# Value projection folded into the output projection's weights, with earlier loads, in a hybrid encoder layer

## The chip, the cores and the metric

The kernel runs on one core of a Trainium2 chip. The metric is the device time of one execution in microseconds. A core has a matrix engine (TensorE, PE in the profile; its weight loads are PEld), a vector engine (VectorE, DVE), a scalar engine (ScalarE, ACT), a general engine (GpSimd, POOL) and an engine that mostly starts transfers (SyncE, SP). Each works through its own list of instructions in order and waits for the others by semaphores. SBUF and PSUM are the memories on the core; PSUM takes the results of matmuls. Transfers (DMA) are issued by an engine, SP for the most part and ACT for some, and run beside the engines.

## The reference

One layer with two kinds of heads, for 2048 tokens of width 1024:

```python
h = rms_norm(x, g_mix_norm)
z = h @ w_in                       # mLSTM q, k, v, out-gate, gates | q-latent (256), kv-latent (128), rotary key (64)
y_a = mlstm_group(...)             # 4 heads, values of 128: convolution of q and k, chunked scans both ways
kv = (rms_norm(c_kv, g_ckv) @ w_ukv).reshape(B, S, 4, 128 + 128)
k_nope, v = kv[..., :128], kv[..., 128:]
s = q . k * scale                  # per head, over all 2048 keys; q and k normalised, 64 of 192 columns rotated
y_b = softmax(s) @ v               # 4 heads, values of 128
x = x + concat(y_a, y_b) @ w_out   # rows 512 to 1023 of w_out belong to y_b, 128 per head
h = rms_norm(x, g_ffn_norm)
x = x + relu(h @ w_ff1)**2 @ w_ff2
```

All is float32. A head's values are a linear map of the normalised latent, `v = cn @ Wv_h`, and the output multiplies a head's result by its 128 rows of `w_out`.

## The kernel before, in words

**Precision.** A float32 matrix product is made of three matmuls on a faster format: each operand is split into a high part (a cast on ACT, L53, or L56 with a gain) and a low part (source minus high, on DVE or POOL, L54, or L57 with a gain), and `mm3` (L68 to L71) adds high x high, high x low and low x high in PSUM. Lines L53 to L57 and L69 to L71 are thus the lines of helpers, and the tile names tell where in the program they are.

**The projection stage** (0 to about 458 us) takes the tokens in two halves of 8 tiles of 128. In each half come a block `rest` (gates and latents), then three blocks of 8 steps: the mLSTM values (`z_v`), its queries and keys with their convolution (`z_qk`: five steps on DVE into acc, a sigmoid sg on ACT, their product ot on DVE at L455, and for the keys transposes on PE, L464 and, for the last two columns, L476), and the out-gate (`z_o`: sigmoid vo on ACT, L495, a product on DVE, a store d_sg issued by ACT, L497). The weights of a block are 8 row blocks, each loaded into a raw tile by SP and split into wh and wl. Beside the blocks `tick` runs the latent attention's preparation for one token tile in four parts. mla_a1 normalises the latents (cn) and transposes them (cTh, cTl). mla_a2 multiplies them with the weights: the kv-latent with the 1024 columns of w_ukv (wukh, wukl), the q-latent with 768. mla_b1 copies the values out of PSUM (vn, L369), stores them in the DRAM tensor d_va (L371) and normalises queries and keys. mla_b2 transposes and stores queries and keys. Input tiles are loaded by SP (`load_x`, L147) into a pool of two buffers and transposed in `prep`. This stage's order on each engine is not written out: a scheduler lays the instructions down by a simulated timeline with priorities (`urgent`).

**The attention stage** (about 458 to 1120 us) is issued as written. It goes over 16 blocks, 4 heads x 4 groups of 512 queries, each of 16 scores (a score is 128 queries by 512 keys: five matmuls, L1090 to L1094, and a reduction on DVE, L1095). One loop of steps g (a score each, 16 per block) issues the scores, the softmax of four scores before (ACT), the transposes of the block before (PE, with casts on ACT and low parts on DVE), the products with the values (`pv`), and one piece of the mLSTM (`work`: a prelude for the gates, L628 to L718, then chunk by chunk). Loads and splits of keys, queries and values for what comes stand at fixed steps: `split_k` of the next head in its last group (two of the last three on POOL, one on DVE), `split_q` on POOL, and `load_v` and `split_v` once per head and quarter, 16 times in all, the low part on POOL. For head 0 the value splits are at steps 6, 8, 10 and 12.

**The output stage** (about 1120 to 2540 us) multiplies the joined results with w_out and then does the feed-forward part, with products of blocks that save multiplications. It reads rows 512 to 1023 of w_out twice, in `weights` and in `load_b2`.

## Time and profile before

| what | value |
|---|---|
| time, median of 3 runs | 2543.32 us (2542.84 to 2547.24) |
| the profiled execution's own time | 2542.08 us |
| its span | 2540.3 us |
| PE busy | 2523.7 us (99%), 12380 instructions |
| DVE, ACT, POOL busy | 1726.1 us (68%), 1293.7 us (51%), 380.7 us (15%) |
| DMA | 392.53 MB, mean 155 GB/s |

The span runs from the first to the last instruction of one profiled execution; the time of an execution is a little longer. A row of the timeline gives start, length, engine, line, operation, and output <- inputs, then partitions x elements and types; in brackets stands how long the engine was idle before and what ended that. A row of the groups ends with busy time, the mean length of one in ns, and the idle time ahead. A row of the waits gives the waiting instruction <- what it waited for: us in total, times, longest.

### The profile page before, as it was taken

The page shows a single profiled execution, that of the slowest core. Times are in us where ns is not written, and L with a number is a line of the kernel's source. Part 1 is how long each engine was busy: PE and PEld are TensorE (multiplying, and loading weights), DVE is VectorE, ACT ScalarE, POOL GpSimd, SP SyncE. Part 2 cuts the span into 40 slices and gives each one's busy share as a digit, 9 for nine tenths or more (in the row PEclk, how much of TensorE's full clock was granted, in tenths as well). Part 3 has the DMA queues.
Part 4 walks back from the last instruction along what each step waited for, and adds up shares of the span by engine and source line. Part 5 has one row for each costly group of instructions (what it writes and reads, how often), then busy time and mean ns, then how long its engine had stood idle before and what let it go on. Part 6 is the DMA issues. An engine that isn't in the chain of part 4 may idle for free. (4 is left out here: it accounts for less than half of the span.)

```text
span 2540.3 us, 35812 instructions
## 1 busy us (share of the span) xinstructions
PE 2523.7 (99%) x12380; PEld 2111.3 (83%) x12380; DVE 1726.1 (68%) x3286; ACT 1293.7 (51%) x2900; POOL 380.7 (15%) x428
## 2 busy tenths in 40 slices
PE   9999999999999999999999999999999999999999
PEld 7888888788888888888888888888888888888887
DVE  5585467766667667678788777977775577665433
ACT  6454444656767677674455555655554323332332
POOL 1211111223323332200000000000000232322000
PEclk9999999999999999999999999999999999999999
DMA  5434234355344343235786555654448544444552
GB/s 177 143 112 152 91 113 137 111 146 134 89 115 114 85 121 102 63 110 193 235 271 227 196 189 185 244 166 149 142 153 300 201 149 142 145 145 145 211 183 95
DMA packets 295931, 392.53 MB, mean 155 GB/s; under 512 B 32262, under 2 KB 176965, under 8 KB 295749
## 3 DMA queue, kind: packets, MB, share of 16 engines
q1 hardware_dynamic: 293284, 385.78, 48.0%
q10 hardware_dynamic: 2464, 4.46, 0.5%
q8 instruction: 97, 1.59, 0.3%
q14 instruction: 86, 0.70, 0.1%
HBM read 258.51 MB, written 131.64 MB: 154 GB/s over the span
## 5 line engine op out<-in xcount | busy, mean ns | idle before, releaser
L69 PE MATMUL pd<-w2h,uh 128*128 128x512 f32 x896 | 348.8, 389 | 0.1
L70 PE MATMUL pd<-w2l,uh 128*128 128x512 f32 x896 | 348.7, 389 | 0.0
L71 PE MATMUL pd<-w2h,ul 128*128 128x512 f32 x896 | 348.7, 389 | 0.0
L54 DVE TENSOR_TENSOR ul<-ur,uh 128x1024 fp32r<-128x1024 f32 x110 | 149.3, 1357 | 251.8 <-ACT uh L53 251.8
L53 ACT CAST uh<-ur 128x1024 fp32r<-128x1024 f32 x110 | 115.7, 1052 | 396.0 <-PE pd L70 382.4
L54 DVE TENSOR_TENSOR ptl<-ptp,pth 128x512 fp32r<-128x512 f32 x248 | 171.1, 691 | 190.0 <-ACT pth L53 188.9
L53 ACT CAST pth<-ptp 128x512 fp32r<-128x512 f32 x248 | 143.4, 578 | 157.7 <-PE ptp L1137 157.1
L2015 DVE TENSOR_TENSOR e<-pu,e 128x512 f32<-128x512 f32 x224 | 151.3, 689 | 88.7 <-PE pu L71 87.7
L69 PEld LDWEIGHTS pd<-w2h,uh 128*128 128x128 f32 x896 | 168.2, 188 | 35.4 <-DVE e L2015 0.5
L71 PEld LDWEIGHTS pd<-w2h,ul 128*128 128x128 f32 x896 | 168.2, 188 | 34.9
L70 PEld LDWEIGHTS pd<-w2l,uh 128*128 128x128 f32 x896 | 168.2, 188 | 34.8
L1106 ACT ACTIVATE p<-p,nm 128x512 f32<-128x512 f32 x256 | 185.8, 726 | 2.6 <-DVE nm L1099 2.6
L1095 DVE TENSOR_SCALAR_CACHE_REDUCE p<-ps 128x512 f32<-128x512 f32 x256 | 167.4, 682 | 15.2 <-PE ps L1094 15.1
L2179 POOL TENSOR_TENSOR r<-wr,r 128x512 f32<-128x512 f32 x48 | 81.5, 1697 | 621.1 <-DMA wr<-in_w 590.0
L69 PE MATMUL pz<-wh,hh 128*128 128x512 f32 (+1 forms) x384 | 149.5, 391 | 1.7 <-ACT vo L495 0.7
L71 PE MATMUL pz<-wh,hl 128*128 128x512 f32 (+1 forms) x384 | 150.0, 391 | 0.0
L70 PE MATMUL pz<-wl,hh 128*128 128x512 f32 (+1 forms) x384 | 149.2, 389 | 0.1
L2018 ACT ACTIVATE e<-e 128x512 f32<-128x512 f32 x128 | 80.9, 632 | 120.5 <-DVE e L2015 114.0
L1137 PE MATMUL ptp<-ident,p 128*128 128x128 f32 x992 | 130.6, 274 | 0.5 <-DVE ptl L54 0.3
L1137 PEld LDWEIGHTS ptp<-ident,p 128*128 128x128 f32 x992 | 113.6, 140 | 14.1 <-issue 1.4
L1090 PE MATMUL ps<-kh,qh 128*128 128x512 f32 x256 | 112.8, 441 | 2.4 <-DVE p L1095 2.4
L1883 ACT CAST r<-w1raw 128x512 fp32r<-128x512 f32 x104 | 64.6, 622 | 92.5 <-PE pu L71 92.5
(526 smaller groups left out, 6463.5 us busy)
## 6 DMA issues: line engine op xcount, KB each, us to landing
d_u<-e SPq DMA_DIRECT2D x224, 256.0 KB
ur<-d_u SPq DMA_DIRECT2D x110, 512.0 KB
wr<-in_w SPq DMA_DIRECT2D x96, 256.0 KB
w1raw<-in_w SPq DMA_DIRECT2D x42, 512.0 KB
raw<-in_w_in SPq DMA_DIRECT2D x48, 256.0 KB
r<-in_w SPq DMA_DIRECT2D x22, 512.0 KB
mb<-d_M SPq DMA_DIRECT2D x32, 256.0 KB
acc<-d_x SPq DMA_DIRECT2D x16, 512.0 KB
```

Source lines behind the costliest of these rows:

```text
L53: r = nc.scalar.copy(hi, src)
L54: (eng or nc.vector).tensor_tensor(lo, src, hi.bitcast(F32), op=ALU.subtract)
L69: nc.tensor.matmul(out, ah, bh, start=first, stop=False, skip_group_check=more)
L70: nc.tensor.matmul(out, ah, bl, start=False, stop=False, skip_group_check=more)
L71: nc.tensor.matmul(out, al, bh, start=False, stop=last, skip_group_check=more)
L1090: nc.tensor.matmul(o, qh[:, qs], kh, start=True, stop=False)
L1095: nc.vector.tensor_scalar(p, o, SCALE, None, op0=ALU.mult, op1=ALU.max, accum_out=maxes[b, a][:, j:j + 1])
L1106: nc.scalar.activation(p, p, AF.Exp, bias=maxes[b, a], accum_out=dens[b][:, a, j:j + 1])
L1137: nc.tensor.transpose(pt[:, k, :], p[:, k * P:(k + 1) * P], c.ident)
L2015: nc.vector.tensor_tensor(out, o, t, op=ALU.add)
L2018: nc.scalar.activation(t, t, AF.Relu)
L2179: nc.gpsimd.tensor_tensor(R, wr, R, op=ALU.subtract)
```

## The change

Since a head's result is softmax(s) times cn times Wv_h, and the output then multiplies by that head's rows of w_out, the kernel now attends with the normalised kv-latent itself (128 wide, the same for all four heads) and multiplies the head's result with `Wv_h @ w_out[head's rows]`, a 512 x 1024 matrix d_wv that it forms once.

- Values: d_va, its copies (vn) and its stores go. mla_a2 stores the latent cn (d_cn, 128 columns) from ACT's queue, and has one product of 512 columns for the keys instead of two for keys and values. Attention loads and splits the 4 quarters of d_cn once, at steps 2 to 8 and 16 to 22, and uses them for all heads.
- `value_rows()`, a generator called once a step in the second half from step n = 11 on, forms d_wv: it loads w_ukv again, scales its value columns with the gain (ACT), transposes them (four on PE), splits them into wvh and wvl, and then multiplies head by head with the pieces of w_out: 8 products of three matmuls, in psM tiles named pm. The pieces 0, 2, 4, 6 are split into a pair wh, wl of the weights' pool, the pieces 1, 3, 5, 7 into the pair acc, sg of the convolution's. The results are copied by ACT to ot or zc and stored from ACT's queue.
- The output stage reads d_wv where it read rows 512 to 1023 of w_out.
- Input tiles: three buffers instead of two. Tiles 8 to 10 are loaded at step i = 3 of the first half's last block, ahead of the weights that follow, and tiles 11 to 15 three tiles ahead.
- In the attention stage one split_k of a head change goes from POOL to DVE, and the mLSTM's chunk loads move: the first four into the prelude, the later ones a step ahead.

```diff
-    c.d_va = dr.tile([S, 512], F32, name="d_va")
+    c.d_cn = dr.tile([S, P], F32, name="d_cn")
+    c.d_wv = dr.tile([NH * P, D], F32, name="d_wv")
...
-        xp = pool("a_x", 2, "right")
+        xp = pool("a_x", 3, "right")
...
+        wvh = gp.tile([P, NH, P], F32R, name="wvh")
+        wvl = gp.tile([P, NH, P], F32R, name="wvl")
...
-                raw = rp.tile([P, 512], F32, name="raw")
-                cs = slice(j * 512, (j + 1) * 512)
-                nc.sync.dma_start(raw, c.w_ukv[:, cs])
-                split(nc, wukh[:, cs], wukl[:, cs], raw, gcq[:, 2:3])
+                raw = load_ukv(j)
+                cs = slice(j * 256, (j + 1) * 256)
+                split(nc, *[w[:, cs].rearrange("p (h d) -> p h d", h=2) for w in (wukh, wukl)],
+                      raw[:, :, 0, :], gcq[:, 2:3])
+
+        def load_ukv(j):
+            raw = rp.tile([P, 512], F32, name="raw")
+            nc.sync.dma_start(raw, c.w_ukv[:, j * 512:(j + 1) * 512])
+            return raw.rearrange("p (h t d) -> p h t d", h=2, t=2)
+
+        def value_rows():
+            raws = [load_ukv(j) for j in range(2)]
+            yield
+            for raw in raws:
+                nc.scalar.activation(raw[:, :, 1, :], raw[:, :, 1, :], AF.Copy, scale=gcq[:, 2:3])
+            pt = psT.tile([P, 4, P], F32, name="pt")
+            for h in range(NH):
+                nc.tensor.transpose(pt[:, h, :], raws[h // 2][:, h % 2, 1, :], c.ident)
+            split(nc, wvh, wvl, pt)
+            yield
+            for _ in range(3):
+                yield
+            pieces, parts = {}, {}
+            homes = [(wp.tile([P, 512], F32R, name="wh"), wp.tile([P, 512], F32R, name="wl")),
+                     [ep.tile([P, 520], F32R, name=name, bufs=1)[:, 0:512] for name in ("acc", "sg")]]
+
+            def load(n):
+                if n < 2 * NH:
+                    h, j = divmod(n, 2)
+                    pieces[n] = rp.tile([P, 512], F32, name="raw")
+                    nc.sync.dma_start(pieces[n], c.w_out[512 + h * P:512 + (h + 1) * P, j * 512:(j + 1) * 512])
+
+            def part(n):
+                if n < 2 * NH:
+                    parts[n] = homes[n % 2]
+                    split(nc, *parts[n], pieces.pop(n))
+                    load(n + 5)
+
+            for n in range(5):
+                load(n)
+            yield
+            part(0)
+            part(1)
+            yield
+            for grp in ((0,), (1,), (2, 3), (4, 5), (6, 7)):
+                for n in grp:
+                    h, j = divmod(n, 2)
+                    o = psM.tile([P, 512], F32, name="pm")
+                    mm3(nc, o, wvh[:, h, :], wvl[:, h, :], *parts.pop(n), True, True)
+                    w = ep.tile([P, 520], F32, name=("ot", "zc")[j])[:, 0:512]
+                    nc.scalar.copy(w, o)
+                    nc.scalar.dma_start(c.d_wv[h * P:(h + 1) * P, j * 512:(j + 1) * 512], w)
+                for n in grp:
+                    part(n + 2)
+                yield
...
-                pk.append(o)
+            zr, ms3, ch, cl, cn = mla_env[t]
+            nc.scalar.dma_start(c.d_cn[t * P:(t + 1) * P, :], cn[:, 256:384])
+            pq = []
+            pk = psM.tile([P, 512], F32, name="pm")
+            mm3(nc, pk, ch[:, 2, :], cl[:, 2, :], wukh[:, 0:512], wukl[:, 0:512], True, True)
...
-            vn = mp.tile([P, NH, DV], F32, name="vn")
-            for j in range(2):
-                nc.scalar.copy(vn[:, 2 * j:2 * j + 2, :],
-                               pk[j].rearrange("p (h d) -> p h d", h=2)[:, :, NOPE:])
-            nc.sync.dma_start(c.d_va[tok, :], vn.rearrange("p h d -> p (h d)"))
...
+            elif 8 <= t < 13:
+                xts[t + 3] = load_x(t + 3)
...
+            rows = value_rows()
...
+                    if half and n >= 11:
+                        next(rows, None)
+                    if half == 0 and blk == 2 and i == 3:
+                        for t in range(8, 11):
+                            xts[t] = load_x(t)
...
+        for ch in grp:
+            if ch > 4:
+                ld[ch - 4] = mlstm_v(c, ch - 4), mlstm_k(c, ch - 4)
         yield
         for k, ch in enumerate(grp):
             new = back[ch - 1] = advance(1, NT - 1 - ch, outs[k])
             if ch > 4:
                 nc.sync.dma_start(c.d_C[ch - 1], new)
-                ld[ch - 4] = mlstm_v(c, ch - 4), mlstm_k(c, ch - 4)
...
-        def load_v(h, j):
-            raw = vraw[h, j] = rp.tile([P, 512], F32, name="raw").rearrange("p (k d) -> p k d", k=4)
-            nc.sync.dma_start(raw, c.d_va[j * 512:(j + 1) * 512, h * DV:(h + 1) * DV].rearrange(
-                "(k p) d -> p k d", p=P))
-
-        def split_v(h, j):
-            raw = vraw.pop((h, j))
+        def load_v(j):
+            raw = vraw[j] = rp.tile([P, 512], F32, name="raw").rearrange("p (k d) -> p k d", k=4)
+            nc.sync.dma_start(raw, c.d_cn[j * 512:(j + 1) * 512, :].rearrange("(k p) d -> p k d", p=P))
+
+        def split_v(j):
+            raw = vraw.pop(j)
             vh = vp.tile([P, 4, DV], F32R, name="vh")
             vl = vp.tile([P, 4, DV], F32R, name="vl")
             split(nc, vh, vl, raw, eng=nc.gpsimd)
-            V[h, j] = vh, vl
+            V[j] = vh, vl
...
-            ld = {ch: (mlstm_v(c, ch), mlstm_k(c, ch)) for ch in range(NT - 1, NT - 5, -1)}
-            yield from mlstm_prelude(c, psM)
+            for n, _ in enumerate(mlstm_prelude(c, psM)):
+                if n == 10:
+                    ld = {ch: (mlstm_v(c, ch), mlstm_k(c, ch)) for ch in range(NT - 1, NT - 5, -1)}
+                yield
...
-        def next_v(bp, j):
-            h = bp // NB + 1
-            if bp % NB == NB - 1 and h < NH:
-                split_v(h, j)
-                if j < 2:
-                    load_v(h, j + 2)
...
-                    split_k(h + 1, u - 3, nc.vector if u == 6 else nc.gpsimd)
-                    if u == 6:
-                        load_v(h + 1, 0)
-                        load_v(h + 1, 1)
+                    split_k(h + 1, u - 3, nc.gpsimd if u == 4 else nc.vector)
...
-                if g in (6, 8, 10, 12):
-                    split_v(0, g // 2 - 3)
-                    if g < 10:
-                        load_v(0, g // 2 - 1)
+                if g in (2, 4, 6, 8):
+                    load_v(g // 2 - 1)
...
-            nc.sync.dma_start(raw, c.w_out[k * P:(k + 1) * P, :])
+            nc.sync.dma_start(raw, c.d_wv[(k - 4) * P:(k - 3) * P, :])
...
-                                     self.c.w_out[(4 + k) * P:(5 + k) * P, half * 512:(half + 1) * 512])
+                                     self.c.d_wv[k * P:(k + 1) * P, half * 512:(half + 1) * 512])
```

The order in which PE reaches the end of the projection stage, before, from the last convolution's transposes on (pz is a projection of the out-gate, ps an attention score):

```order
L464 MATMUL pt<-ident,ot 128x128 x4
L476 MATMUL pt<-ident,ot 2x128
L70 MATMUL pz<-wl,hh 128x512
L71 MATMUL pz<-wh,hl 128x512
L69 MATMUL pz<-wh,hh 128x512
L70 MATMUL pz<-wl,hh 128x512
L71 MATMUL pz<-wh,hl 128x512
L1094 MATMUL ps<-rl,qr 128x512
L1090 MATMUL ps<-kh,qh 128x512
```

and with the change (its own line numbers, so L464 is now L510; pm is a product for d_wv, and the names behind it are its operands):

```order
L510 MATMUL pt<-ident,ot 128x128 x4
L522 MATMUL pt<-ident,ot 2x128
L69 MATMUL pm<-acc,wvh 128x512
L69 MATMUL pm<-wh,wvh 128x512
L70 MATMUL pm<-wl,wvh 128x512
L71 MATMUL pm<-wh,wvl 128x512
L70 MATMUL pm<-sg,wvh 128x512
L71 MATMUL pm<-acc,wvl 128x512
L69 MATMUL pm<-acc,wvh 128x512
```

The transposes now stand behind the last projection, and seven products (21 matmuls, of which these are the first seven) follow before the first score; product 0 stands among the projections ahead.

On ACT, from the cast of piece 1 of the output weights (the first acc) on, these rows stand with the change:

```order
L53 CAST acc<-raw 128x512
L541 ACTIVATE vo<-pz 128x512
L512 COPY kt<-pt 128x512
L53 CAST wh<-raw 128x512
L543 DMA d_sg<-vo 128x512
L319 COPY zc<-pm 128x512
L53 CAST acc<-raw 128x512
L319 COPY ot<-pm 128x512
L320 DMA d_wv<-zc 128x512
L320 DMA d_wv<-ot 128x512
L319 COPY ot<-pm 128x512
L53 CAST wh<-raw 128x512
```

and further on, up to the casts of the last pieces:

```order
L524 COPY kt<-pt 2x128
L319 COPY zc<-pm 128x512
L53 CAST acc<-raw 128x512
L320 DMA d_wv<-ot 128x512
L320 DMA d_wv<-zc 128x512
L319 COPY ot<-pm 128x512
L320 DMA d_wv<-ot 128x512
L319 COPY zc<-pm 128x512
L53 CAST acc<-raw 128x512
```

The casts into the two pairs alternate with the copies of the products and their stores; none of these rows was there before, apart from vo, kt and d_sg.

More of the change, by code (lines that the diff above doesn't have):

```diff
@@ L329, in mla_a1 @@
                 split(nc, ch, cl, pt[:, 0:3, :])
-            mla_env[t] = [zr, ms3, ch, cl]
+            mla_env[t] = [zr, ms3, ch, cl, cn]
         def mla_a2(t):
-            zr, ms3, ch, cl = mla_env[t]
-            pk, pq = [], []
-            for j in range(2):
-                o = psM.tile([P, 512], F32, name="pm")
-                cs = slice(j * 512, (j + 1) * 512)
-                mm3(nc, o, ch[:, 2, :], cl[:, 2, :], wukh[:, cs], wukl[:, cs], True, True)
-                pk.append(o)
+            zr, ms3, ch, cl, cn = mla_env[t]
[3 more added lines that the diff above has]
+            mm3(nc, pk, ch[:, 2, :], cl[:, 2, :], wukh[:, 0:512], wukl[:, 0:512], True, True)
             for j in range(2):
@@ L350, in mla_a2 @@
             qs = [pq[h // 2][:, (h % 2) * DH:(h % 2 + 1) * DH] for h in range(NH)]
-            ks = [pk[h // 2][:, (h % 2) * 256:(h % 2) * 256 + NOPE] for h in range(NH)]
+            ks = [pk[:, h * NOPE:(h + 1) * NOPE] for h in range(NH)]
             for h in range(NH):
@@ L360, in mla_a2 @@
             rsqrt(c, r8, ms8, 8)
-            mla_env[t] = [zr, pk, qs, ks, r8]
+            mla_env[t] = [zr, qs, ks, r8]
         def mla_b1(t):
-            tok = slice(t * P, (t + 1) * P)
-            zr, pk, qs, ks, r8 = mla_env[t]
-            vn = mp.tile([P, NH, DV], F32, name="vn")
-            for j in range(2):
-                nc.scalar.copy(vn[:, 2 * j:2 * j + 2, :],
-                               pk[j].rearrange("p (h d) -> p h d", h=2)[:, :, NOPE:])
-            nc.sync.dma_start(c.d_va[tok, :], vn.rearrange("p h d -> p (h d)"))
+            zr, qs, ks, r8 = mla_env[t]
             kpe = mp.tile([P, 1, ROPE], F32, name="kpe")
@@ L1141, in pv @@
         def pv(b, j, k):
-            h = b // NB
             if (j, k) == (0, 0):
@@ L1145, in pv @@
             th, tl = pts[b, j]
-            vh, vl = V[h, j]
+            vh, vl = V[j]
             if b < N - 1:
@@ L1239, in attention @@
                         load_k(h + 1, u - 3)
-                if g in (6, 8, 10, 12):
-                    split_v(0, g // 2 - 3)
-                    if g < 10:
-                        load_v(0, g // 2 - 1)
+                if g in (2, 4, 6, 8):
+                    load_v(g // 2 - 1)
+                if g in (16, 18, 20, 22):
+                    split_v(g // 2 - 8)
             if g0 == 16 * N - 10:
```

4 lines of the change are left out of this document (removed).

## The prediction

> **What bounds the kernel now.** I read the page's first two parts, then who TensorE (PE) waited for, then the timeline of PE around the end of the projection stage, and last DVE, ACT and POOL there.
>
> ```profile
> span 2540.3 us, 35812 instructions
> PE 2523.7 (99%) x12380; PEld 2111.3 (83%) x12380; DVE 1726.1 (68%) x3286; ACT 1293.7 (51%) x2900; POOL 380.7 (15%) x428
> PEclk9999999999999999999999999999999999999999
> PE pt L204 <- DMA rows<-in_g_mix: 4.5, 1, 4.5
> PE ps L1090 <- DVE p L1095: 2.4, 4, 1.3
> PE pt L325 <- DVE cn L321: 1.4, 1, 1.4
> PE pz L69 <- ACT vo L495: 0.7, 1, 0.7
> ...
> PE pz L69 <- ACT hh L53: 0.6, 2, 0.3
> PE pz L69 <- ACT wh L56: 0.4, 1, 0.4
> ```
>
> PE is idle for 2540.3 - 2523.7 = 16.6 us of the span, 4.5 us of it at the start, and all its waits are short. So the time is the sum of what PE has to issue, plus whatever wait a change adds to it. A matmul's duration is not its price, though. Rows of PE's timeline at the tail of the projections, where nothing waits:
>
> ```profile
> 440.25 0.39 PE L69 MATMUL pz<-wh,hh 128*128 128x512 f32 x1
> 440.48 0.39 PE L70 MATMUL pz<-wl,hh 128*128 128x512 f32 x1
> 440.71 0.39 PE L71 MATMUL pz<-wh,hl 128*128 128x512 f32 x1
> ...
> 444.79 0.39 PE L71 MATMUL pz<-wh,hl 128*128 128x512 f32 x1
> 445.01 0.39 PE L1090 MATMUL ps<-kh,qh 128*128 128x512 f32 x1
> ```
>
> Each is 0.39 us long, but the next starts 0.23 us later (0.227 over the whole stretch: 20 matmuls of this shape start from 440.25 on, before the one at 444.79). A 128x512 matmul more or less costs 0.227 us of PE; its result is ready 0.39 us after its start.
>
> **The change, part by part. Matmuls removed.** In the projection stage each of 16 token tiles projects its 128 latents to 1024 columns, keys and values, in two triples of matmuls (the third line, L71, is in the same count):
>
> ```profile
> L69 PE MATMUL pm<-wukh,cTh 128*128 128x512 f32 x32 | 13.0, 408 | 0.0
> L70 PE MATMUL pm<-wukl,cTh 128*128 128x512 f32 x32 | 12.6, 394 | 0.0
> ```
>
> Now one triple of the two is left: 48 matmuls go, 48 x 0.227 = 10.9 us. Attention's products keep their shapes, since the latent has 128 columns as a head's values have, and so do the output's.
>
> **Matmuls added.** Eight products of a head's value weights with half a row block of the output weights, three matmuls each: 24 x 0.227 = 5.45 us. Four transposes of 128x128; four such take PE 449.08 - 448.64 = 0.44 us:
>
> ```profile
> 448.64 0.60 PE L464 MATMUL pt<-ident,ot 128*128 128x128 f32 x4
> 449.08 0.27 PE L476 MATMUL pt<-ident,ot 128*2 128x128 f32 x1
> ```
>
> PE's own work thus falls by 10.9 - 5.45 - 0.44 = 5.0 us.
>
> **The wait that this adds.** The question is what PE does while it forms those products. The two pieces of PE's order shown with the change give the place: before, the projections run straight into the first scores; now all projections are over, and seven of the eight products (21 matmuls, 4.77 us) stand in a row ahead of the first score. Only product 0 is earlier, and nothing else stands between them to cover a wait. Their operands have two homes, wh with wl and acc with sg, so a piece of output weights can be cast only when the product before it in that home is done. The piece of ACT's order shown there sets the pace: each new acc stands behind a cast of wh and a copy of the last product on ACT. Rows for these kinds, on ACT, DVE (the low part) and ACT's issue of a store:
>
> ```profile
> 433.84 0.60 ACT L495 ACTIVATE vo<-pz 128x512 f32<-128x512 f32 x1
> 434.33 0.59 ACT L466 COPY kt<-pt 128x512 f32<-128x512 f32 x1
> ...
> 438.72 0.62 ACT L53 CAST kh<-raw 128x512 fp32r<-128x512 f32 x1
> 439.24 0.62 ACT L53 CAST rh<-raw 128x512 fp32r<-128x512 f32 x1
> ...
> 459.73 0.33 ACTq L497 DMA_DIRECT2D d_sg<-vo  x1
> 460.18 0.26 ACT L478 COPY kt<-pt 2x128 f32<-2x128 f32 x1 [1.42 <-DMA d_k<-kt]
> ```
>
> ```profile
> 441.47 0.69 DVE L54 TENSOR_TENSOR kl<-raw,kh 128x512 fp32r<-128x512 f32 x1
> 442.08 0.68 DVE L54 TENSOR_TENSOR rl<-raw,rh 128x512 fp32r<-128x512 f32 x1
> ```
>
> A copy holds ACT 0.49 us and a cast 0.52 (ready after 0.62); the small copy 0.24, a store's issue 0.33; a low part is ready after 0.69. Count from the start of the first matmul of an acc product. The even product's three matmuls come next (0.227, 0.454, 0.681) and end at 0.681 + 0.39 = 1.07; the acc product's own end at 1.135 + 0.39 = 1.53. First round: cast wh to 1.59, copy to 2.08, cast acc ready at 2.70. Second: copy from 1.07 to 1.56, cast wh to 2.08, small copy to 2.32, copy to 2.81, cast ready at 3.43. Third: copy to 1.56, its store issued once it has ended (1.66 + 0.33 = 2.0), copy to 2.49, cast ready at 3.1. Last: the low part after 0.69, two matmuls, and the first score at 1.15. Handovers of some 0.03 us each bring it to 2.75 + 3.45 + 3.15 + 1.15 = 10.5 us for 4.77 us of work: **5.75 us of waiting**. Bounds: with copy and cast alone between rounds (1.53 + 0.49 + 0.62 = 2.64, three times, + 1.15) it is 9.1 us, 4.3 of waiting; with full lengths instead of steps (11 ACT rows x 0.1) and five exposed issues x 0.33 it is 13.2, 8.4 of waiting. None at all if the next piece were always ready, which two homes exclude.
>
> Is the chain's start ready in time? Its first cast needs the last convolution's result, which lets go of acc and sg:
>
> ```profile
> 453.37 0.75 DVE L455 SCALAR_TENSOR_TENSOR ot<-acc,cb,sg 128x514 f32<-128x514 f32 x1 [0.86 <-ACT sg L452]
> ...
> 457.96 0.39 PE L1094 MATMUL ps<-rl,qr 128*128 128x512 f32 x1
> ```
>
> PE reaches the scores at 457.96, having done four of their matmuls earlier (one is the row at 445.01 above): 457.05 in effect. Now it reaches the first of the seven products at 457.05 - 10.9 + 0.44 + 0.68 (product 0) = 447.3. The convolution ended at 454.1; moved ahead by the same 10.5 us, and with three low parts more on DVE in front of it (3 x 0.61), it ends at 445.4, so acc is cast by 446.2. In time by 1.1 us. Scores then begin at 447.3 + 10.5 = 457.8 instead of 457.05.
>
> **Value loads and splits.** DVE slows beside POOL; the page has the pair:
>
> ```profile
> 468.23 0.28 DVE L647 TENSOR_TENSOR d<-d,wi 128x128 f32<-128x128 f32 x1
> 468.62 1.20 DVE L649 TENSOR_TENSOR ln<-ln,d 128x128 f32<-128x128 f32 x1
> ...
> 471.25 0.50 PE L1090 MATMUL ps<-kh,qh 128*128 128x512 f32 x1 [0.69 <-DVE p L1095]
> 480.30 0.50 PE L1090 MATMUL ps<-kh,qh 128*128 128x512 f32 x1 [1.34 <-DVE p L1095]
> ```
>
> ```profile
> 468.37 1.30 POOL L54 TENSOR_TENSOR vl<-raw,vh 128x512 fp32r<-128x512 f32 x1 [13.25 <-PE ps L1094]
> L54 POOL TENSOR_TENSOR vl<-raw,vh 128x512 fp32r<-128x512 f32 x16 | 20.6, 1285 | 80.2 <-ACT vh L53 58.8 <-PE ps L1094 13.2 <-DMA mb<-d_M 7.9
> ```
>
> A split of values (vl, POOL) ran over DVE's L649 and made it 0.9 us longer, and PE waited 0.69 us for the reduction behind. These splits move from the sixth to the sixteenth score on: I take the 0.69 us away, and leave the 1.34, which follows eight short scans whose place is the same. Twelve of sixteen value splits vanish, off PE's path. One key split per head goes from POOL to DVE, 2 x 0.69 us, three times; DVE has about a third of that stage free. I put it at 0, at most 3 x 1.38 = 4.1 us.
>
> **Tiles loaded ahead and earlier chunk loads.** The input tiles of the second half wait for buffers on SP, with weights behind them, yet PE's waits on the weights and the tiles (wh and hh in its list) are 1.0 us in the whole run. 0, between -1 and +1. The mLSTM chunk loads move ahead by a step of work that PE never waits for: 0.
>
> **Sum.** -5.0 + 5.75 - 0.69 = +0.06 us on the profiled 2542.08 us (its span and 1.8 us around it). The median of the runs is 1.24 us above that execution: 2543.4 us.
>
> **The clock.** Early matmuls are slow: eight transposes take 1.97 us at the start and 1.04 later,
>
> ```profile
> 4.69 1.97 PE L163 MATMUL pt<-ident,xt 128*128 128x128 f32 x8
> ...
> 41.30 1.04 PE L163 MATMUL pt<-ident,xt 128*128 128x128 f32 x8
> ```
>
> and a wait of 1.34 us (above) left the score behind it at 0.50 us. The added waits are up to 2 us each, between short bursts. The Trainium skill ("TensorE: Matmul & The Clock Gate", "What's actually happening") says that PE falls back to half its rate after an idle window of about 3.4 us; by that rule waits this short leave the rate alone, and only a longer one would cost. No run here shows such a fall yet.
>
> **The rivals.** (1) *The waits are covered*: casts and copies keep up, and the 5.0 us saved stay, with the 0.69: 2543.3 - 5.7 = 2537.6 us, faster. For it: ACT is busy 51%, DVE 68%. Against: the two homes. (2) *The chain starts late*: if DVE doesn't move ahead with PE, since it has more to do in that stretch than the other helpers (its busy time, its share of 35 us and its instructions),
>
> ```profile
> 425.00:460.00 35.00, 27.47 (x53) 1.00 0.73 212
> ```
>
> the last convolution ends at 454.1 + 1.8 = 455.9, the first cast at 456.7, and the scores start at 467.2, 9.4 us later than I say: 2552.8 us. It costs from 446.5 on, microsecond for microsecond, and makes the kernel slower by 0.2% once the convolution ends after 451. Against: DVE's waits on PE and on ACT's casts of loaded keys, in that stretch, come from work that moves with PE. (3) *The rate falls in the gaps*: 21 product matmuls 1.9 times as slow (1.97 / 1.04, above), 0.9 x 4.77 = +4.3 us, 2547.7 us, or over 2548.4 if the first scores are slow too. (4) *The change does less than it says*, as the tiles loaded ahead do in my sum: already at 0.
>
> **How the numbers follow.** Forecast 0.63; (1) 0.17; (2) 0.15; (3) 0.05, half of it past the bound. 0.2% (5.1 us) is about what a measurement of this kernel tells from no change. Faster 0.17; slower 0.15 + 0.03 = 0.18; the same 0.65. Predicted 2543.4 us. The forecast's own bounds are -1.5 (short chain) to +2.7 (long chain), with up to 4.1 for the key splits; taking in (1) and half of (2), 2537 to 2550 us.
>
> **What would show it.** PE busy down by about 5 us and PE waits up by as much; PE idle rows on the products of the value weights, for DVE and ACT, about 1.5 to 2.3 us each, at 448 to 458 us; scores starting at about 457.8; the wait at 471 gone. Wrong: products back to back; the first product waiting for acc long after 447; waits on the reduction at the three head changes; transposes at 0.2 us each after the products.

## The result and the profile after

The changed kernel takes 2553.16 us (median of 7 runs, 2550.99 to 2554.46) against 2544.23 us of the kernel before beside it (7 runs): 1.0031 times as long, interval 1.002 to 1.0043. I had forecast 2543.4 us, no change, in a range up to 2550. It is slower, by about what my rival 2 gave (2552.8 us). The kernel before was measured again beside each batch of runs; its medians lie between 2544.2 and 2545.4 us, so a difference between runs of two batches is good to about 1 us, and the ratios and intervals below go by the kernel before of the same batch. The profiled execution took 2553.84 us, its span 2551.7; the two profiled executions are 11.8 us apart, the medians 8.9. Its page, and its list of PE's waits:

```profile
span 2551.7 us, 35725 instructions
PE 2525.8 (99%) x12360; PEld 2111.6 (83%) x12360; DVE 1732.5 (68%) x3301; ACT 1292.5 (51%) x2875; POOL 364.3 (14%) x410
```

```profile
PE pm L69 <- ACT acc L53: 4.8, 3, 1.9
...
PE pt L510 <- DVE ot L501: 3.1, 1, 3.1
PE pz L69 <- ACT vo L541: 2.3, 2, 2.2
...
PE ps L1145 <- DVE p L1150: 0.4, 1, 0.4
```

PE has fewer matmuls and yet a larger busy time. Three waits stand there that the kernel before did not have in this size: for the cast of an odd piece of the output weights (acc, 4.8 us), for the last convolution's result (ot, 3.1) and for a sigmoid of the out-gate (vo, 2.3 instead of 0.7). The wait for the score reduction fell from 2.4 to 0.4. PE's timeline at the end of the projections, with the waits in brackets:

```profile
454.35 1.11 PE L510 MATMUL pt<-ident,ot 128*128 128x128 f32 x4 [3.10 <-DVE ot L501]
455.25 0.42 PE L522 MATMUL pt<-ident,ot 128*2 128x128 f32 x1
455.33 0.77 PE L69 MATMUL pm<-acc,wvh 128*128 128x512 f32 x1
...
459.05 0.50 PE L69 MATMUL pm<-acc,wvh 128*128 128x512 f32 x1 [1.24 <-ACT acc L53]
...
462.58 0.50 PE L69 MATMUL pm<-acc,wvh 128*128 128x512 f32 x1 [1.87 <-ACT acc L53]
...
466.00 0.80 PE L69 MATMUL pm<-acc,wvh 128*128 128x512 f32 x1 [1.68 <-ACT acc L53]
...
467.74 0.63 PE L1145 MATMUL ps<-kh,qh 128*128 128x512 f32 x1
468.17 0.63 PE L1146 MATMUL ps<-kl,qh 128*128 128x512 f32 x1
468.59 0.63 PE L1147 MATMUL ps<-kh,ql 128*128 128x512 f32 x1
```

The scores begin at 467.74 us, 10.7 later than the 457.05 of before. From there to the end it is 2551.7 - 467.74 = 2084.0 us, against 2540.3 - 457.05 = 2083.2 before. So the loss is made before the first score. Of the 10.7 us, -5.0 are the matmuls saved and added; +4.8, +3.1 and +1.6 are the three waits; and the last rows show one thing more: matmuls 0.43 us apart instead of 0.227. The windows of PE give its busy time and the granted clock (the column behind it):

```profile
400.00:405.00 5.00, 3.55 (x10) 0.76 0.22 56
...
450.00:455.00 5.00, 1.90 (x9) 0.88 1.06 315
455.00:460.00 5.00, 3.76 (x14) 0.78 1.04 359
460.00:465.00 5.00, 2.44 (x10) 0.90 0.53 200
465.00:470.00 5.00, 4.00 (x9) 0.50 0.56 194
```

The clock fell to half in 465 to 470 us, and it had done so once before, behind the wait for the sigmoid (2.17 us at 401.45): some 8 matmuls at 0.43 us in 402.9 to 405.9, and about 13 after 455, each 0.2 us late. That is 21 x 0.2 = 4.2 us, of which 7 x 0.2 = 1.4 lie behind the first score. -5.0 + 9.5 + 2.8 = 7.3; the other 3.4 of the 10.7 us are spread over short waits and over matmuls that start late behind a wait, which I did not assign one by one.

The wait for the sigmoid is the products' too. On ACT the cast of the first piece of the output weights waits for its load, and a token's statistics and then the sigmoid stand behind it; PE's row of the wait and one of the slow matmuls follow:

```profile
395.26 0.62 ACT L53 CAST wh<-raw 128x512 fp32r<-128x512 f32 x1 [1.23 <-DMA raw<-in_w_out]
...
400.82 0.58 ACT L541 ACTIVATE vo<-pz 128x512 f32<-128x512 f32 x1
```

```profile
401.45 0.50 PE L69 MATMUL pz<-wh,hh 128*128 128x512 f32 x1 [2.17 <-ACT vo L541]
...
402.87 0.63 PE L71 MATMUL pz<-wh,hl 128*128 128x512 f32 x1
```

Why the convolution came late: the cast of attention's first queries (qh) held ACT for 5.3 us until a store had landed, with a sigmoid of the convolution (sg) behind it, and the convolution after that, the last one, waited for its turn of the buffers acc and sg. ACT's row of the cast, and what followed it, then DVE's end of the last convolution:

```profile
439.16 0.62 ACT L53 CAST qh<-raw 128x512 fp32r<-128x512 f32 x1 [5.30 <-DMA d_k<-kt]
439.69 0.72 ACT L498 ACTIVATE sg<-acc,vec 128x514 f32<-128x514 f32 x1
```

```profile
453.53 0.76 DVE L501 SCALAR_TENSOR_TENSOR ot<-acc,cb,sg 128x514 f32<-128x514 f32 x1
```

The profile names the store that landed last, that of kt; which stores the place of qh had to wait for comes out in the third round. The convolution ended at 454.3 us, where before it ended at 454.1. PE was done with its projections at 451.1 us, some 6 us sooner than before, and DVE and ACT had not moved with it.

### The profile page after: what moved, and what is told of

It is laid out like the page before. It is cut to its first block, busy times and chain, and to the rows that moved or that the text cites. A ratio compares the mean times of both kernels' runs of the same rounds, so it can differ in the third digit from the quotient of the medians.

```text
span 2551.7 us, 35725 instructions
## 1 busy us (share of the span) xinstructions
PE 2525.8 (99%) x12360; PEld 2111.6 (83%) x12360; DVE 1732.5 (68%) x3301; ACT 1292.5 (51%) x2875; POOL 364.3 (14%) x410
```

## The experiments

My theory A after this: all of the loss stands at the end of the projection stage. Its rivals: that the loss is the convolution's lateness alone, or that part of it lies in attention, or in the loads ahead.

### First round: parts taken away, homes added

**no_products.** In the second half `next(rows, None)` is left out and the output stage reads the output weights.

```diff
                     if half and n >= 11:
-                        next(rows, None)
+                        pass
...
-            nc.sync.dma_start(raw, c.d_wv[(k - 4) * P:(k - 3) * P, :])
+            nc.sync.dma_start(raw, c.w_out[k * P:(k + 1) * P, :])
...
-                                     self.c.d_wv[k * P:(k + 1) * P, half * 512:(half + 1) * 512])
+                                     self.c.w_out[(4 + k) * P:(5 + k) * P, half * 512:(half + 1) * 512])
```

> The change without forming the folded weights: no pieces, no products, and the output stage reads the output weights as they are, so the output is not the reference's (the factor of the value weights is left out). Theory A (all of the loss stands at the end of the projection stage, where the products wait for their operands and run at a lower clock): the 48 matmuls saved stay, 10.9 us, and nothing is lost; 2544.2 - 10.9 - 0.7 = 2532.6 us, scores starting at about 446 to 449 us. Rival B (the loss is mostly that the last convolution ends at 454.3 us whatever PE does, since ACT and DVE are held by the loads of queries and keys): PE stands before the scores until then, 2538 to 2541 us. Rival C (part of the loss lies in the attention stage, by the one shared latent or the moved key split): above 2541 us.

Measured: 2536.90 us, 0.9964 (0.9951 to 0.9976). That is between A and B. PE still waits for the last convolution, less long, since it can start scores first:

```profile
PE pt L510 <- DVE ot L501: 1.6, 1, 1.6
```

So the matmuls saved are worth 8.5 us beside the kernel before and not 10.9 + 0.7, and forming the folded weights costs 2553.16 - 2536.90 = 16.3 us, where their matmuls and transposes are 5.9. The waits for the sigmoid are 0.8 us in all here, instead of 2.3.

**odd_home_moved.**

```diff
+            xt = xp.tile([P, D], F32R, name="xt")
...
-                     [ep.tile([P, 520], F32R, name=name, bufs=1)[:, 0:512] for name in ("acc", "sg")]]
+                     (xt[:, 0:512], xt[:, 512:D])]
```

> The odd pieces of the output weights go into one tile of the input tiles' pool, which is free by then, in place of the convolution's acc and sg; still two homes. Theory A1 (the chain of products starts late because acc is held by the last convolution until 454.3 us): the products start when PE has the projections done, some 3 to 5 us earlier; 2548 to 2550 us. Rival A2 (the pace of the chain is all, two homes and ACT between the rounds, whenever it starts): the waits for the cast stay 4.8 us, and the convolution's own transposes still wait; 2552 to 2554 us.

Measured: 2548.78 us, 1.0011 (1.0002 to 1.002). That is in A1's range: some 4 us come from the odd pieces' home in acc and sg. The move changes the order too: four of the products stand behind the last projection instead of seven. Waiting for the convolution and standing behind it are thus not told apart.

**four_homes.**

```diff
-            homes = [(wp.tile([P, 512], F32R, name="wh"), wp.tile([P, 512], F32R, name="wl")),
-                     [ep.tile([P, 520], F32R, name=name, bufs=1)[:, 0:512] for name in ("acc", "sg")]]
+            homes = [(wp.tile([P, 512], F32R, name="wh"), wp.tile([P, 512], F32R, name="wl"))]
+            for _ in range(3):
+                xt = xp.tile([P, D], F32R, name="xt")
+                homes.append((xt[:, 0:512], xt[:, 512:D]))
...
-                    parts[n] = homes[n % 2]
+                    parts[n] = homes[n % 4]
...
-            part(0)
-            part(1)
+            for n in range(4):
+                part(n)
...
-                    part(n + 2)
+                    part(n + 4)
```

> Four homes for the pieces: wh with wl, and three tiles of the input tiles' pool; none shared with the convolution, four pieces cast before the first product. Theory A (waiting for homes and for the convolution, and the clock that falls with it): acc waits of 4.8 us go, the clock stays up for the products, about 3 to 4 us more, and the wait for the last convolution (3.1 us) is covered by products; 2541 to 2545 us, waits of PE in the transition under 3 us. Rival B (the convolution's end paces the transition whatever the homes): 2548 to 2551 us.

Measured: 2548.18 us, 1.0011 (1.0002 to 1.002): no more than the one home moved, and in the range of B, though not by its reason: PE no longer waits for the last convolution. In its order all eight products stand among the projections. The waits on pieces are gone, but others stand in their place, the largest of them on ACT:

```profile
PE pz L69 <- ACT vo L543: 3.5, 2, 3.4
PE ps L1147 <- ACT kh L53: 2.1, 1, 2.1
...
PE pm L684 <- ACT vo L543: 1.0, 1, 1.0
```

Behind the wait of 3.4 us for the sigmoid 14 matmuls run 0.43 us apart, some 2.8 us more.

**no_tiles_ahead.**

```diff
-        xp = pool("a_x", 3, "right")
+        xp = pool("a_x", 2, "right")
...
-            elif 8 <= t < 13:
-                xts[t + 3] = load_x(t + 3)
...
-                    if half == 0 and blk == 2 and i == 3:
-                        for t in range(8, 11):
-                            xts[t] = load_x(t)
```

> The change with two buffers for input tiles and without the three tiles loaded ahead; all else as it is. My sum had 0 for this part: 2553 us, between 2552 and 2554. Rival D (the loads ahead do help PE at the start of the second half): 1 us or more above. Rival E (the late loads of the out-gate's weights, and the 2.2 us that PE waits at 401 us for the sigmoid, come from moving loads on SP's queue): 2 us less, 2551 us or below.

Measured: 2545.58 us, 1.0001 (0.9992 to 1.001). The part that stood at 0 in my sum is worth 7.6 us, all of the loss but about 1 us. Not through the loads' help at the start of the second half: that is lost here (hh, 3.1 us), and PE waits 3.0 us for the sigmoid, so that rival E has the number without its reason. But acc is 1.2 instead of 4.8, and the wait for the convolution is gone:

```profile
PE pz L69 <- ACT hh L53: 3.1, 3, 1.9
PE pz L69 <- ACT vo L541: 3.0, 1, 3.0
PE pm L69 <- ACT acc L53: 1.2, 1, 1.2
```

The last convolution on DVE, and on ACT the cast that had waited 5.3 us, now without a wait:

```profile
441.92 0.74 DVE L501 SCALAR_TENSOR_TENSOR ot<-acc,cb,sg 128x514 f32<-128x514 f32 x1
```

```profile
428.17 0.73 ACT L498 ACTIVATE sg<-acc,vec 128x514 f32<-128x514 f32 x1 [2.27 <-DVE acc L495]
428.80 0.60 ACT L53 CAST qh<-raw 128x512 fp32r<-128x512 f32 x1
```

It ends at 442.7 us, 11.6 sooner than in the change; my working had 445.4. The question was now what in the tiles loaded ahead makes it late.

### Second round: the loads ahead, the third buffer, the products

**before_tiles_ahead.** The three buffers and the loads ahead in the kernel before, with the same lines as in the diff of the change.

> The kernel before with the tiles loaded ahead alone (three buffers, tiles 8 to 10 at step 3 of the first half's last block, the rest three tiles ahead). Theory S (the loads ahead cost only together with the products: they let PE reach the end of the projections sooner, while the last token tile's latent work and the convolutions stay late, and only the products have to wait for these): no loss here, 2543 to 2546 us. Rival T (the loads ahead cost by themselves, 7.6 us as in the pair of the change and the change without them): 2550 us or above. By my prediction 0, the same range as S.

Measured: 2545.20 us, 0.9997 (0.9988 to 1.0006): S. By themselves they cost nothing, although the last convolution ends late there too (458.9 us): with no products, scores stand ahead of its transposes.

**three_buffers_only.** The change with three buffers, without the loads at step i = 3 and without `xts[t + 3]`.

> The change with three buffers for input tiles, but without the loads ahead. Rival P (the third buffer alone moves the other tiles of that side, and the query and key tiles of attention then come to lie where something is freed late: the cast of the first queries waited 5.3 us in the changed kernel and none without the third buffer): 2551 to 2553 us. Theory S (it is when the loads are issued that counts): 2545 to 2547 us, as with two buffers.

Measured: 2554.04 us, 1.0032 (1.0021 to 1.0043). So it isn't the loads; the third buffer alone, with the products there, makes the whole loss. The same waits are back:

```profile
PE pm L69 <- ACT acc L53: 5.1, 3, 2.5
...
PE pt L510 <- DVE ot L501: 3.4, 1, 3.4
PE pz L69 <- ACT vo L541: 2.6, 2, 2.5
```

Two things come with a third buffer. It moves the tiles that follow on its side by 4 KB: with two buffers the first qh lies where the transposed keys and queries (kT, qT) lay, with three where the rotated parts (rT) lay, which are stored last. And the scheduler makes another order. The place of four things in PE's order, counted in matmuls of the 1536 of the projections (pz) that stand ahead:

| | kernel before | change, three buffers | change, two buffers |
|---|---|---|---|
| last token tile's transposes of rotated parts | 1440 | 1462 | 1414 |
| last convolution's transposes | 1531 | 1536 | 1498 |
| products 1 and 2 | | 1536 | 1500 |
| products 3 and 4 | | 1536 | 1527 |
| products 5 to 7 | | 1536 | 1536 |

With two buffers 36 projection matmuls, 8.2 us of PE's work, still stand behind products 1 and 2, and cover the waits of the next pieces. With three none does.

**two_buffers_three_homes.** No tiles ahead, homes wh with wl and two tiles xt; `parts[n] = homes[n % 3]`.

> The change without the tiles loaded ahead, and with three homes for the pieces: wh with wl, and the two tiles of the input tiles' pool, three pieces cast before the first product. Theory A (waits for homes, then little else): the products come to lie among the projections, the 1.4 us of waits on acc and sg go, and more of the 5.0 us saved shows: 2540 to 2544 us, below the kernel before. Rival B (ACT and DVE behind loads pace the stage whatever the homes): 2545 to 2548 us.

Measured: 2546.92 us, 1.0006 (0.9997 to 1.0015): B. The products lie among the projections in the order, and PE waits on none of them; it waits 3.9 us for the sigmoid instead:

```profile
PE pz L69 <- ACT vo L543: 3.9, 1, 3.9
PE pz L69 <- ACT hh L53: 1.7, 3, 1.0
```

**two_buffers_no_products.** As no_products, without the tiles ahead.

> The change without the tiles loaded ahead and without forming the folded weights; the output stage reads the output weights as they are, so the output is not the reference's (the factor of the value weights is left out). It gives the price of the products where the tiles are not loaded ahead: 24 matmuls and 4 transposes are 5.9 us, the waits on acc and sg 1.4 us; 2545.6 - 7.3 = 2538.3 us (2537 to 2540) if they cost no more than that. Rival: the pieces' loads and casts hold up ACT too (PE waited 3.0 us for a sigmoid behind the first piece's cast), 2535 us or below.

Measured: 2535.83 us, 0.9962 (0.995 to 0.9975). The products cost 2545.58 - 2535.83 = 9.8 us here, 3.9 more than their matmuls; that is between the two numbers expected, nearer to the rival's. Of the waits, acc and the 3.0 us for the sigmoid go with them.

### Third round: the place of a tile, or the order

Exchanging the lines that allocate qh and ql exchanges their places in SBUF and leaves the order of every engine as it was, row by row. In each kernel:

```diff
-            qh = qp.tile([P, 512], F32R, name="qh")
             ql = qp.tile([P, 512], F32R, name="ql")
+            qh = qp.tile([P, 512], F32R, name="qh")
```

**swapped_places**, on the changed kernel, and **two_buffers_swapped**, its counterpart:

> The changed kernel with the places of two tiles exchanged and nothing else: the low part of the first queries (ql, on DVE) now lies where the rotated parts of the last token tile (rT) lay, and the high part (qh, cast on ACT) on cTh, which is free long before. The order on every engine is the same row by row. Theory P1 (the third buffer costs because it moves qh onto rT, so that the cast waits 5.3 us on ACT for rT's stores, with the convolution's sigmoid behind it): the last convolution ends some 5 us sooner, the 3.1 us of PE for it go and part of the slow matmuls, 2545 to 2549 us. Rival P2 (it is the order that the scheduler makes with three buffers, the last token tile later on every engine): 2552 to 2554 us.

> The counterpart: the change without the tiles loaded ahead and with two buffers, the same two tiles exchanged, so that here qh comes to lie on rT; the order on every engine is that of the two-buffer kernel, row by row. Theory P1: the cast of qh waits for rT's stores (copied at 424 us, stored by about 430 us), and what stands behind it on ACT and DVE comes later by as much, some 1 to 3 us; 2547 to 2551 us. Rival P2 (the order): 2545 to 2546 us, as without the exchange.

Measured: 2551.40 us, 1.0032 (1.002 to 1.0044), and 2545.75 us, 1.0003 (0.9994 to 1.0012). The mechanism of P1 is there, its size is not. In the changed kernel qh's cast waits no longer for a store, and starts at 435.42 instead of 439.16; in the kernel with two buffers it now does wait. The row of each, the changed kernel's first:

```profile
435.42 0.62 ACT L53 CAST qh<-raw 128x512 fp32r<-128x512 f32 x1 [2.24 <-DVE acc L495]
```

```profile
433.01 0.62 ACT L53 CAST qh<-raw 128x512 fp32r<-128x512 f32 x1 [1.85 <-DMA d_k<-kt]
```

The wait moves with the place of rT, so it is for the stores of rT, though the profile names that of kt. In swapped_places the last convolution ends 2.1 us sooner, and the scores start at 465.28 instead of 467.74. But PE waits 6.1 us for acc instead of 4.8, and in the time no gain can be told: the medians differ by 1.8 us, the ratios to the kernel before of the batch (1.0031 and 1.0032) not at all, and their intervals would allow some 4 us. So by the medians the place explains little or nothing of the 7.6 us, and the order is left for most of it (P2). That is by exclusion: no run changes the order and nothing else. Why the scheduler, which only sees times of its own, orders the last token tile later with three buffers, these runs do not tell.

**four_homes_swapped.** The exchange on four_homes.

> Four homes for the pieces and the same exchange, with three buffers and the tiles loaded ahead. Theory P1 (wait of 4.6 us of qh's cast on ACT goes, and with it the 2.1 us that PE waits for the cast of keys behind it): 2543 to 2546 us. Rival P2: 2548 us as without the exchange. Any time under 2542 us would be faster than the kernel before.

Measured: 2546.89 us, 1.0011 (1.0002 to 1.002). No gain that can be told from four_homes.

### Fourth round: the products elsewhere

**early_products_two_buffers** and **early_products_tiles_ahead**: the products begin at the second half's first step, among the projections of the values, with the homes of two_buffers_three_homes and of four_homes. Of the edit:

```diff
-                    if half and n >= 11:
+                    if half:
                         next(rows, None)
```

> Two buffers, three homes, and the products begun at the first step of the second half's value block instead of step 11 (without the three idle steps between): in the order of PE they lie among the projections of that block, no projection's wait for the last convolution stands before the scores, and the scores begin among the last projections. Theory O (what costs is where the order puts the products: at the end they have nothing to cover the waits for their operands): the products cost their 24 matmuls and 4 transposes, 5.9 us, on top of the 2535.8 us of the kernel with two buffers and without products: 2541 to 2543 us, faster than the kernel before by some 3 us, about what can be told. Rival L (their loads and casts hold ACT and SP wherever they stand, as the 3 to 4 us that PE waited for a sigmoid): 2545 us or above.

> The same early products with three buffers, four homes and the tiles loaded ahead, as in the change. Theory O: 2541 to 2544 us: the products add 5.9 us to the 2536.9 us of the change without them, or less, since the wait of 1.6 us for the last convolution goes too. If the third buffer or the loads ahead cost by themselves: 2547 us or above. Rival L: 2547 us or above too, but then the kernel with two buffers is at 2545 or above as well.

Measured: 2570.83 us, 1.0103 (1.0087 to 1.0119), and 2569.83 us, 1.0093 (1.0079 to 1.0108). My theory that order alone decides was wrong by 27 to 29 us here. PE waits, in the kernel with two buffers, for the next block's weights, for the copy ahead of a convolution and for the normalised latents:

```profile
PE pz L69 <- ACT wh L56: 7.9, 5, 2.9
PE pz L69 <- ACT zc L487: 6.1, 2, 5.0
...
PE pt L379 <- DVE cn L375: 4.4, 3, 2.6
```

The pieces take the raw buffers of the weights, a home among their tiles, and ACT. My reading, which no run takes apart, is that this stage has work on PE to cover the products, but not the buffers and the ACT time for their operands.

**fold_in_attention** (two buffers) and **fold_in_attention_tiles_ahead**: `value_rows` is out of the projection stage. A generator in attention does one piece at a time in the last head's blocks, every second score a step (load; cast and low part; three matmuls; copy and store), in the fifth buffer of the keys' pool, which is free there.

```diff
+            for n in range(2 * NH):
+                h, j = divmod(n, 2)
+                raw = rp.tile([P, 512], F32, name="raw")
+                nc.sync.dma_start(raw, c.w_out[512 + h * P:512 + (h + 1) * P, j * 512:(j + 1) * 512])
+                yield
+                split(nc, hi, lo, raw)
+                yield
+                o = psM.tile([P, 512], F32, name="pm")
+                mm3(nc, o, wvh[:, h, :], wvl[:, h, :], hi, lo, True, True)
+                yield
+                w = rp.tile([P, 512], F32, name="raw")
+                nc.scalar.copy(w, o)
+                nc.sync.dma_start(c.d_wv[h * P:(h + 1) * P, j * 512:(j + 1) * 512], w)
```

> Two buffers, no tiles ahead, and the folded weights formed in the last head's part of the attention stage in place of the projection stage: one step of the work (load, split, three matmuls, copy and store of one piece in turn) every second score, in buffers of the keys' pool that are free there; one home is enough at that pace. Theory O2 (the products cost more than their matmuls only for lack of work to cover their operands; in attention PE has scores and transposes for that): 2535.8 us of the kernel without products + 24 x 0.227 + 0.44 = 2541.7 us, 2540 to 2543.5, faster than the kernel before by 2 to 4 us. Rival L2 (ACT's casts and copies and DVE's low parts make the softmax late there): 2545 us or above, with PE waits on the score reductions or the transposes' casts.

> The same with three buffers and the tiles loaded ahead, as in the change. Theory O2: 2536.9 + 5.9 = 2542.8 us, 2541 to 2544.5. If the third buffer's order costs even without products in the projection stage: 2546 us or above (the kernel without products says no).

Measured: 2549.14 us, 1.0016 (1.0007 to 1.0025), and 2549.59 us, 1.002 (1.0011 to 1.0029). The times are in L2's range, but not by its reason: the softmax isn't late, but PE waits at the mLSTM's outputs (num), four times:

```profile
PE pm L918 <- ACT num L924: 7.0, 4, 1.8
```

The mLSTM has two PSUM tiles (psM), and a product held one of them over a whole step.

**fold_in_attention_own_slot** (two buffers) and **fold_in_attention_own_slot_ahead**: the generator is called twice a step, the matmuls at a step's end and the copy at the next one's start.

> As the fold in attention with two buffers, but the three matmuls of a product stand at the end of a step and its copy at the start of the next, so that its PSUM tile is held only where the mLSTM's steps take none of the two. In the run before, PE waited 4 times, 7.0 us in all, at the mLSTM's outputs for a PSUM tile that the product held. Theory O2 with that mended: 2549.1 - 7.0 = 2542 us, 2540.5 to 2544, faster than the kernel before. Rival L2 (ACT and DVE have no room for the product's operands): 2546 us or above, PE waiting elsewhere instead.

> The same with three buffers and the tiles loaded ahead: 2549.6 - 7.0 = 2542.6 us, 2541 to 2544.5, by theory O2; 2546 us or above by rival L2.

Measured: 2546.84 us, 1.0005 (0.9996 to 1.0014), and 2549.70 us, 1.0015 (1.0006 to 1.0024). With two buffers 2.3 us better, with three nothing that can be told. The wait has moved to the product itself, which takes the tile next:

```profile
PE pm L69 <- ACT num L924: 3.0, 3, 1.3
...
PE pm L1249 <- ACT num L924: 0.9, 1, 0.9
PE pm L69 <- ACT pth L53: 0.9, 1, 0.9
```

**fold_in_attention_score_banks** (two buffers). The order is the last kernel's row by row; the PSUM tile of the products (and of the four transposes ahead of them) is one of the scores' three.

```diff
-                o = psM.tile([P, 512], F32, name="pm")
+                o = psS.tile([P, 512], F32, name="ps")
```

> The last kernel with two buffers again, its order the same row by row; a product's PSUM tile is one of the three of the scores in place of one of the two of the mLSTM. In the run before PE still waited 4.8 us for the mLSTM's results to be copied out of the tile that the product takes next. Theory O2: these 4.8 us go and nothing takes their place; 2546.8 - 4.8 = 2542.0 us, 2540.5 to 2543.5, faster than the kernel before by about 3 us. Rival L2: the scores' reductions then free their tiles too late, PE waits on DVE there instead, 2545 us or above.

Measured: 2541.73 us, 0.9987 (0.9978 to 0.9996): O2, within 0.3 us of the number expected, and the only one of the folded kernels that is faster than the kernel before, by 2.7 us beside it, a small gain whose interval ends just below 1 (11.4 us below the change). PE's waits in it, behind the one at the start, and a product in its place (kh and kl are here the parts of the piece, rh and rl those of the value weights, and the last row is a score):

```profile
PE pz L69 <- ACT hh L53: 3.0, 3, 1.9
PE ptp L1184 <- DVE ptl L54: 0.9, 2, 0.6
```

```profile
980.45 0.39 PE L920 MATMUL pm<-Cb,iz 128*128 128x129 f32 x2
980.59 0.48 PE L69 MATMUL ps<-kh,rh 128*128 128x512 f32 x1
980.90 0.40 PE L70 MATMUL ps<-kl,rh 128*128 128x512 f32 x1
981.13 0.39 PE L71 MATMUL ps<-kh,rl 128*128 128x512 f32 x1
981.36 0.39 PE L1137 MATMUL ps<-kh,qh 128*128 128x512 f32 x1
```

A product stands between an mLSTM step and a score at PE's usual spacing. The price of all eight is 2541.73 - 2535.83 = 5.9 us, as the prediction counted for 24 matmuls and 4 transposes; with each of the two taken beside the kernel before of its own batch it is 9.4 - 2.7 = 6.7 us, so the agreement to a tenth is chance, and that to 1 us is not. In what is left PE still waits 3.0 us for the tiles of the second half (hh); a version with these loaded ahead and the score banks was not run.

## Why the prediction was wrong, step by step

- **Matmuls removed and added** (-5.0 us): right. Where no wait comes with it the added part costs 5.9 to 6.7 us (last run), and of the removed 10.9 us 8.5 to 9.4 are seen in the kernels without products.
- **The wait that this adds** (10.5 us from the first of the seven products to the first score, 4.77 of it work): right in kind, the two homes and ACT between rounds. It measured 467.74 - 455.33 = 12.4 us. The three waits for acc were 1.24, 1.87 and 1.68 us, 4.8 in all; some 2 us of slow matmuls, and late starts behind the waits, make up the rest. What I left out is the wait for the sigmoid at 401 us, 1.6 us longer than before, with 8 slow matmuls behind it, which comes from the load of the first piece.
- **"The convolution ended at 454.1; moved ahead by the same 10.5 us"**: this step failed. It ended at 454.3, 8.9 us later than my 445.4, and so PE waited 3.1 us for it, and the row of products began at 455.33 instead of 447.3. I let DVE and ACT move with PE because their waits in that stretch came from work that moves with PE; but the order put the last token tile's steps, and with them the loads of queries and keys, later behind a faster PE (1462 instead of 1440 projection matmuls ahead), and the cast of qh held ACT for a store. Without the third buffer and the loads ahead the step holds: the convolution ended at 442.7 us (no_tiles_ahead). The outcome was that of rival 2, to which I gave 0.15: scores at 467.2 us, 2552.8 us. Its reason was another: it had DVE busy with more work of its own, where DVE stood idle for 3.3 us behind ACT's cast of qh. Its number is close in part by luck, since a convolution that ended 1.6 us sooner than it says, a chain 1.9 us longer than mine and the sigmoid's wait came together.
- **"Tiles loaded ahead ... 0, between -1 and +1"**: this step failed with it. The loads are worth 0 by themselves (before_tiles_ahead), but the third buffer turns the order and costs 7.6 us together with the products. I had weighed the transfers and SP's queue, not what a pool's size does to the places of later tiles and to the scheduler's order. With two buffers the kernel takes 0.2 us more than the kernel before, as my sum has it (+0.06), but not by its path: products stand among projections there, PE waits 1.2 us for acc instead of 5.75, and 3.0 us for the sigmoid and 3.1 us for hh come in. That agreement is luck.
- **The clock**: "waits this short leave the rate alone" failed. No single wait was above 3.1 us, yet the clock was 0.50 in 465 to 470 us. The Trainium skill ("TensorE: Matmul & The Clock Gate", "What's actually happening") gives the fall after an idle window of about 3.4 us. The spacing of 0.43 us agrees with its half rate; the length of the wait does not. One wait of 2.17 us was enough at 401 us, and three of 1.2 to 1.9 us with 1.4 us of work between them were enough ahead of 466. Nor does the length of a wait decide: swapped_places, with waits up to 2.6 us and the same order, kept 1.00 from 455 us on, and three_buffers_only went on at 0.227 us behind one of 3.41 us. What decides, these runs don't show. Rival 3, to which I gave 0.05, thus came in part, 4.2 us in all; but of the 21 slow matmuls only 6 are products.
- **Value splits and key splits** (-0.69, and 0): right in size. The wait on score reductions fell from 2.4 to 0.4 us, so the 1.34 us that I left in went too, and where the scores start at the full clock the rest of the program is 1.1 us shorter (no_tiles_ahead: 2543.7 - 461.53 = 2082.2, before 2083.2).
- **Rival 1**, that the waits are covered, does not hold anywhere in the projection stage: two kernels without waits on pieces (four_homes, two_buffers_three_homes) wait on ACT for the sigmoid instead. In attention 2.7 of its 5.7 us come true, once the products have PSUM tiles that nobody is short of.

## What to carry to other kernels

When work on the busiest engine is saved, ask of each wait behind it whether what it waits for moves too: here PE gained 6 us on a convolution that stayed where it was, and the gain turned into a wait. Under a scheduler a pool's size is not a local edit: compare where the late work stands in the order of the engine that waits, and try the size alone. Added products belong where the busy engine has other work behind them and where their buffers, PSUM tiles above all, are not the ones that the neighbours turn over.

## What the runs showed of the hardware

The matmul clock can fall to half behind waits of PE that are under 3 us. Single waits of 2.17 us (the change, 401 us), 2.33 us (swapped_places) and 2.82 us (odd_home_moved) were each followed, 0.8 to 1.4 us after PE went on, by about 8 matmuls 0.43 us apart, some 3.4 us in all; three waits of 1.24, 1.87 and 1.68 us with 1.4 us of matmuls between each two (the change, 459 to 466 us) were followed by slow matmuls until 470.7, through the first score and into the second. A longer wait did not always do it: behind 2.49 and 3.41 us (three_buffers_only) and 3.02 us (no_tiles_ahead) the next matmuls stayed 0.23 us apart. Each kernel has one profiled execution, so these runs don't tell whether the same kernel would show a fall each time. Apart from that a 128x512 matmul cost 0.227 us in rows of its own kind wherever it had an operand ready, in the projections as between scores.
